# Dummy products on a constant tile, a clamp on ScalarE, and the sample rows' copies in a stream of their own: three small edits to a planned hybrid decoder layer

## The chip, the core and the metric

The kernel runs on one core of a Trainium2 chip. A core has five engines that run side by side: TensorE (PE: matrix products; its weight loads are shown apart as PEld), VectorE (DVE), ScalarE (ACT), GpSimd (POOL) and SyncE (SP), which here issues the transfers. The metric is the time of one execution on the device in microseconds (us); lower is better. Of several runs the median counts.

## The reference: one layer of a hybrid decoder

One layer is computed for a prompt of 1024 new tokens and, with the same weights, for 8 sample sequences of one new token each that bring their states along. The model width is 1024. The layer projects the input by a wide matrix `w_in`, feeds two branches, and merges them:

```python
p = x @ w_in
q, k, v, g_a, a_lr = gla part of p         # gated linear attention, 4 heads of 128 x 256
pr = p_rwkv + (prev - p_rwkv) * mu          # token shift, then RWKV-7, 16 heads of 64
r, kb, vb, g_b, w_lr, aa_lr = parts of pr
w = exp(-0.606531 * sigmoid(w0 + tanh(w_lr) @ w2));  a = sigmoid(a0 + aa_lr @ a2)
kk = kb * k_k
kk = kk / max(sqrt(sum(kk * kk per head)), 1e-12)
S_t = S_{t-1} (diag(w_t) - kk_t^T (kk_t * a_t)) + v_t^T k_t;   y_t = S_t r_t
m = sigmoid(gate_a) * (o_gla @ w_up_gla) + sigmoid(gate_b) * (o_rwkv @ w_up_rwkv)
y_out = layernorm(2**0.25 * x + m @ w_out)
```

All outputs are float32: the tokens' results, both branches' final states and the last projected row, for the prompt and for the samples. For this change three lines matter: the normalisation of `kk` with its lower bound, the product with `w_out` for the sample rows, and the fact that everything begins with the product by `w_in`.

## The kernel before

**Two passes.** The tokens are treated in two passes of 512 (line 29): pass 0 holds the first 512 prompt tokens and, behind them, the 8 sample tokens (columns 512 to 519, `HT:`); pass 1 the other 512. Data lie with channels on the 128 partitions and tokens along the row. A product in float32 is done as three products of shortened operands: each matrix is split into a high part (a cast on ScalarE) and a low part (the rest, a subtraction on VectorE), and high by high, high by low and low by high are summed. So the tiles `xh`, `xl` are the input's parts, 8 slices of each (`k`), and `wb` holds both parts of half a block of weights (from `wraw`).

**Blocks of products.** `blocks` (line 678) walks a list that `make_plan` wrote: for each block of 128 output columns and each slice `k` three products per column tile, then an evacuation out of PSUM by ScalarE and VectorE. After the projections of both passes come the up-projections, and at the end `out` (line 1554), the product by `w_out`, row block by row block, each followed by `out_part`: residual sum, layer norm and a transfer.

**Who sets the order.** The order on every engine is written out at build time. Each piece of work is a Python generator, a stream, that yields one step at a time. `Order.run` (line 368) keeps a model of when each engine and tile is free; in every round it looks at the next step of all streams and emits the one with the earliest start, less a bonus for the stream's kind (`PRIO`, line 77), plus a charge if the step needs another of ScalarE's function tables (`SETS`, line 84: Sigmoid and Tanh in one, Exp and Ln in another; functions outside that list are taken to need none). A table is loaded at line 392. Steps of `E` may go to VectorE or GpSimd and steps of `C` to ScalarE or VectorE, whichever the model has free first. The engines then run their own queues in that fixed order. A stream's next step is only considered once its last is emitted. Since almost all steps are emitted through one helper, the profile shows them under line 219 and they are told apart by their tiles.

**The start.** `setup` (line 485) makes the constant tiles and sets five bias columns (line 520) and the tile `reset` on VectorE, before the planner begins. The stream `warm` (line 1730) then takes a work tile `z` of 128 x 256, sets it to zero on VectorE and does three float32 products of it on TensorE, whose result nobody reads. In the trace each of them is two instructions, `big<-row`. Meanwhile the first slices of the input and of the weights land (`row<-xT`, `wraw<-w_in`), are split, and the first projections and the low-rank products (`big<-xh,war`, `low_rank`, line 731) begin. The tile `smp` (line 538) is allocated in `setup` and holds the sample rows of the token shift later on.

**A pair's front.** The RWKV heads are treated as 8 pairs per pass, so 16 times in all. `front` (line 1094) prepares a pair. It squares the keys (ScalarE), sums them per head by a product with a block matrix (`head_sums`, line 472, which yields a PSUM bank), clamps the sums from below to 1e-24 on VectorE into the tile `te` (line 1134), and takes the power of -1/2 by Ln and Exp on ScalarE (lines 1138 and 1139). In the trace the clamp is `TENSOR_SCALAR row<-big`, and the Exp is `row<-row,b_kkl`. Between the clamp and the Ln the stream yields a prefix scan on VectorE and a memset. The result is used by a product on VectorE with the tile `nkk`. After the front come a triangular inverse on VectorE and a chain of small products through the tokens.

**The sample rows of the output.** In pass 0, `out` sets in the row block of the 8 sample tokens as the second of five. It collects their columns of the high parts in columns 0 to 7 of a tile `both`, those of the low parts in columns 32 to 39, for each of the 8 slices, so that one pair of products serves both. In the first half of the output columns, each slice's two copies are yielded just before that slice's two products (lines 1583 and 1584), in the stream of the blocks itself; the second half finds them made.

Of the kernel before, what the change touches and what calls it, by code (L numbers as in the profile page):

```python
# [10 lines left out]
F32 = mybir.dt.float32  # L11
# [3 lines left out]
AF = mybir.ActivationFunctionType  # L15
ALU = mybir.AluOpType
# [4 lines left out]
P = 128  # L21
D = 1024
NK = D // P
TP = 1024
NS = 8
T = TP + NS
HT = TP // 2
# [4 lines left out]
NPAIR = RH // 2  # L32
# [61 lines left out]
KK_SCALE = 65536.0  # L94
# [318 lines left out]
class Kern(Order):  # L413
# [71 lines left out]
    def setup(self):  # L485
        nc, a = self.nc, self.a
        E = mybir.EngineType
        self.es.enter_context(self.tc.manual_schedule(engines={E.PE, E.Activation, E.DVE, E.Pool, E.SP}))
        cp = self.pool("const")
        wp = self.pool("w", side="left")  # L490
        self.dr = self.pool("dr", space=DRAM)
        pp = self.pool("psum", space=PSUM)
        xp = self.pool("x", side="right")
        self.r1 = r1 = self.pool("work", side="left")
        for tag, bufs in BANKS.items():
            self.buffers(tag, bufs, lambda tag=tag, bufs=bufs: pp.tile([P, 512], F32, name=tag, bufs=bufs))
        for tag, (shape, bufs) in SBUF.items():
            dt = F32R if tag in PARTS else F32
            self.buffers(tag, bufs, lambda tag=tag, shape=shape, bufs=bufs, dt=dt:
                         r1.tile(shape, dt, name=tag, bufs=bufs))  # L500
        for tag, (shape, bufs) in WBUF.items():
            dt = F32 if tag == "wraw" else F32R
            self.buffers(tag, bufs, lambda tag=tag, shape=shape, bufs=bufs, dt=dt:
                         wp.tile(shape, dt, name=tag, bufs=bufs))
        for k in range(NK):
            for v in "hl":
                tag = f"x{v}{k}"
                self.buffers(tag, 1, lambda tag=tag: xp.tile([P, HALF], F32R, name=tag, bufs=1))
        nc.scalar.preload_act_table_set(EXP)
        self.cons = cp.tile([P, CST_W], F32, name="cons")  # L510
        self.pv = cp.tile([P, PV_W], F32, name="pv")
        self.ident = self.cst("ident")
        self.omu = cp.tile([P, NRC], F32, name="omu")
        self.oka = cp.tile([P, 8], F32, name="oka")
        self.nkk = cp.tile([P, 8], F32, name="nkk")
        self.bias = {}
        for n, v in [("glaeps", GLA_EPS), ("gneps", GN_EPS), ("lneps", LN_EPS), ("one", 1.0),
                     ("kkl", 0.5 * math.log(KK_SCALE))]:
            t = cp.tile([P, 1], F32, name="b_" + n)
            nc.vector.memset(t, v)  # L520
            self.bias[n] = t
        dbg = getattr(self, "dbg", {})
        self.o_gla = dbg.get("o_gla", None) or self.dr.tile([D, T], F32, name="o_gla")
        self.o_rwkv = dbg.get("o_rwkv", None) or self.dr.tile([D, T], F32, name="o_rwkv")
        self.sg = [[[self.dr.tile([P, PASS[i][1]], F32, name=f"sg{i}{n}{k}") for k in range(NK)] for n in range(2)]
                   for i in range(2)]
        self.mg = [[self.dr.tile([P, PASS[i][1]], F32, name=f"mg{i}{k}") for k in range(NK)] for i in range(2)]

        self.lev = cp.tile([P, MASKED * 64 * NGC + P], U8, name="lev")

        self.onesr = cp.tile([P, P], F32R, name="onesr")
        self.headsr = cp.tile([P, P], F32R, name="headsr")
        self.war = cp.tile([P, NK * 32], F32R, name="war")
        self.alr = cp.tile([96, HALF], F32R, name="alr")
        self.gw2 = cp.tile([96, GH * GDK], F32R, name="gw2")
        self.GS = [self.dr.tile([P, GDV], F32, name=f"GS{h}") for h in range(GH)]

        self.smp = cp.tile([P, 4, NPAIR, NS], F32, name="smp")
        self.RS = self.dr.tile([4, NS, D], F32, name="RS")
        self.WA = self.dr.tile([2, NS, D], F32, name="WA")  # L540
        self.tail = cp.tile([P, NS + 1, NRC], F32, name="tail")
        self.carry = cp.tile([P, NRC], F32, name="carry")
        self.shT = cp.tile([P, NRC, NS], F32, name="shT")
        self.reset = cp.tile([P, HT], U8, name="reset")
        nc.vector.memset(self.reset, 1)
        nc.vector.memset(self.reset[:, ::C], 0)

        self.Sd = [self.dr.tile([P, C], F32, name=f"Sd{n}") for n in range(NPAIR)]

        for tag, n, bufs in (("az", 4 * HT, 2), ("XT", 2 * HT, 2), ("Lp", HT, 1), ("As", HT, 1)):  # L550
            ts = [cp.tile([P, n], F32, name=f"{tag}{i}") for i in range(bufs)]
            for t in ts if tag != "az" else []:
                nc.gpsimd.memset(t, 0.0)
            self.fixed(tag, ts)
# [539 lines left out]
    def front(self, c, p, st, d):  # L1094
        a, A, V, E = self.a, self.A, self.V, self.E
# [24 lines left out]
        ta, tb, td, te, Pc_ = yield from self.rows(5)  # L1120
        ta, tb, td, te = (x[:, :HT] for x in (ta, tb, td, te))
# [9 lines left out]
        yield A.activation(td, pa, AF.Sigmoid, bias=self.pvec("a0", p))  # L1131
        self.free(pa, l2)
        ps = yield from self.head_sums(te)
        yield V.tensor_scalar(te, ps, 1e-24, None, ALU.max)
        self.free(ps)
        yield V.tensor_tensor_scan(tb, self.reset, ta, 0.0, ALU.mult, ALU.add)
        yield E.memset(Pc[:, :, 0:1], 1.0)
        yield A.activation(te, te, AF.Ln, scale=KK_SCALE)
        yield A.activation(te, te, AF.Exp, scale=-0.5, bias=self.bias["kkl"])
        yield A.activation(Pc[:, :, 1:], bc(tb), AF.Exp, scale=-LAM)  # L1140
        yield A.activation(tb, tb, AF.Exp, scale=LAM)
# [13 lines left out]
        ps = yield from self.head_sums(te)  # L1155
# [398 lines left out]
    def out(self, c, xs):  # L1554


        rows = [(n * P, P, slice(0, P), c.i * HT + n * P) for n in range(HT // P)]
        if c.ns:
            rows.insert(1, (HT, C, slice(0, NS), TP))
            both_ = yield from self.row(NK * C)  # L1560
            both = both_.rearrange("p (k t) -> p k t", k=NK).bitcast(F32R)
            yield self.E.memset(both_, 0.0)
        for t0, m, ro, x0 in rows:
            fin = x0 == rows[-1][3]
            w = ro.stop - ro.start
            z_ = yield from self.get("XT")
            z = [z_[ro, :512], z_[ro, 512:]]
            for j in range(2):
                yield self.S.dma_start(z[j], self.a["x"][x0:x0 + w, 512 * j:512 * j + 512])
            st = yield from self.get("st")  # L1570
            end = fin and c.i
            parts = [(0, 512), (512, 256), (768, 256)] if end else [(0, 512), (512, 512)]
            for n, (c0, cn) in enumerate(parts):
                ps = yield from self.get_of("proj", "pY", "big")
                q = ps[:m, :cn]
                j, cs = c0 // 512, slice(c0 % 512, c0 % 512 + cn)
                for k in range(NK):
                    yield lambda: len(xs) > k and len(self.wo) > k
                    hi, lo = (x[j][:, cs] for x in self.wo[k])
                    xh, xl = xs[k]  # L1580
                    if x0 == TP:
                        if not n:
                            yield self.C.copy(both[:, k, 0:NS], xh[:, HT:])
                            yield self.C.copy(both[:, k, 32:32 + NS], xl[:, HT:])
                        yield self.P.matmul(q, both[:, k], hi, start=(k == 0), stop=False)
                        yield self.P.matmul(q, both[:, k], lo, start=False, stop=(k == NK - 1))
                        continue
                    yield self.P.matmul(q, xh[:, t0:t0 + m], hi, start=(k == 0), stop=False)
                    yield self.P.matmul(q, xh[:, t0:t0 + m], lo, start=False, stop=False)
                    yield self.P.matmul(q, xl[:, t0:t0 + m], hi, start=False, stop=(k == NK - 1))  # L1590
                    if fin and n == len(parts) - 1:
                        self.free(xh, xl)

                if x0 == TP and n == len(parts) - 1:
                    self.free(both_)
                self.spawn(self.out_part(n, len(parts), z, j, cs, ps, q[ro], st[ro], ro, x0, [z_, st]), "evacuate")
# [120 lines left out]
    def run_all(self):  # L1717
# [10 lines left out]
        self.make_plan()  # L1728

        def warm():  # L1730
            z = yield from self.row(2 * P)
            yield self.V.memset(z, 0.0)
            ps = yield from self.bank("big", [P, 2 * P])
            for n in range(3):
                yield self.P.matmul(ps, z[:, :P], z, start=True, stop=True)
            self.free(z, ps)
        self.spawn(warm(), "x")

        def samples():
# [59 lines left out]
```

## Time and profile before

| what | value |
|---|---|
| median of 3 runs | 1514.6 us (1512.83 to 1515.94) |
| the profiled execution | 1520.49 us |
| its span, first to last instruction | 1518.7 us |
| instructions | 31506 |
| TensorE products, weight loads | 1481.2 us, 1303.4 us busy |
| VectorE, ScalarE | 1125.9 us, 877.4 us busy |
| mean granted TensorE clock | 0.997 |

The profile shows, for one execution, when each instruction of each engine ran. A stretch row gives the busy time of the engines within a window; a wait row gives how long an engine stood idle and which engine's write of which tile ended that; a row of a group gives the count, total and mean duration of instructions of one shape, and the idle time before them; a timeline row gives the start, the duration and, in brackets, the idle time before it. In names like `row<-big` the written tile stands first; `row` is a general work tile, and `proj`, `big`, `pch` and `pY` are PSUM banks.

### The profile page before, as it was taken

The page shows a single profiled execution, that of the slowest core. Times are in us where ns is not written, and L with a number is a line of the kernel's source. Part 1 is how long each engine was busy: PE and PEld are TensorE (multiplying, and loading weights), DVE is VectorE, ACT ScalarE, POOL GpSimd, SP SyncE. Part 2 cuts the span into 40 slices and gives each one's busy share as a digit, 9 for nine tenths or more (in the row PEclk, how much of TensorE's full clock was granted, in tenths as well). Part 3 has the DMA queues.
Part 4 walks back from the last instruction along what each step waited for, and adds up shares of the span by engine and source line. Part 5 has one row for each costly group of instructions (what it writes and reads, how often), then busy time and mean ns, then how long its engine had stood idle before and what let it go on. Part 6 is the DMA issues. An engine that isn't in the chain of part 4 may idle for free.

```text
span 1518.7 us, 31506 instructions
## 1 busy us (share of the span) xinstructions
PE 1481.2 (98%) x11352; PEld 1303.4 (86%) x11352; DVE 1125.9 (74%) x2570; ACT 877.4 (58%) x2209; POOL 94.5 (6%) x273
## 2 busy tenths in 40 slices
PE   8999999999999999999999999899999999999997
PEld 7999999999999998877878777778788899988786
DVE  5687789786986698669778888776765775665665
ACT  5666677675677577566664555456546645554310
POOL 1010000000110000001001010200000000000000
PEclk9999999999999999999999999999999999999999
DMA  8768977789768976586576557555764778697622
GB/s 305 259 226 263 308 259 220 221 245 308 238 210 251 309 249 218 175 245 178 162 199 209 148 164 234 170 142 176 200 194 127 217 241 260 238 312 252 208 84 83
DMA packets 252823, 330.58 MB, mean 218 GB/s; under 512 B 125011, under 2 KB 148700, under 8 KB 252668
## 3 DMA queue, kind: packets, MB, share of 16 engines
q1 hardware_dynamic: 252668, 328.58, 69.7%
q8 instruction: 90, 1.47, 0.4%
q14 instruction: 65, 0.53, 0.1%
HBM read 198.35 MB, written 118.61 MB: 209 GB/s over the span
## 4 chain that ended last, share of the span: by engine, by line
PE 74%; DVE 13%; DMA 6%; ACT 3%; issue 2%; SPq 1%; POOL 0%; POOLq 0%; DVEq 0%; ACTq 0%
PE proj L219 45%; PE big L219 16%; PE pY L219 8%; DVE row L219 6%; PE pch L219 5%; DVE X L219 3%; ACT row L219 2%; SPq L219 1%; DVE wide L219 1%; DMA row<-sg 1%; DMA wide<-LD 1%; DVE part L219 1%; DMA w<-wb 1%; DVE pair L219 1%; DMA row<-state_rwkv 0%
## 5 line engine op out<-in xcount | busy, mean ns | idle before, releaser
L219 PE MATMUL proj<-xh,wb 128*128 128x256 f32 (+3 forms) x3744 | 912.7, 328 | 1.1 <-DVE row L219 0.8
L219 PEld LDWEIGHTS proj<-xh,wb 128*128 128x128 f32 x3744 | 624.4, 189 | 46.5 <-issue 2.6
L219 PE MATMUL proj<-xl,wb 128*128 128x256 f32 (+3 forms) x1872 | 612.1, 327 | 0.0
L219 PEld LDWEIGHTS proj<-xl,wb 128*128 128x128 f32 x1872 | 353.8, 189 | 23.2 <-issue 1.9
L219 DVE TENSOR_TENSOR wb<-wraw,wb 128x512 fp32r<-128x512 f32 x208 | 141.9, 689 | 78.1 <-ACT wb L219 74.3
L219 ACT CAST wb<-wraw 128x512 fp32r<-128x512 f32 x210 | 129.9, 622 | 90.3 <-PE proj L219 41.1
L219 DVE TENSOR_TENSOR row<-row 128x512 f32<-128x512 f32 (+8 forms) x338 | 166.1, 501 | 15.3 <-DMA row<-state_rwkv 6.4
L219 ACT ACTIVATE row<-row 128x512 f32<-128x512 f32 (+3 forms) x229 | 138.6, 611 | 36.2 <-DVE row L219 17.7
L219 DVE SCALAR_TENSOR_TENSOR wide<-pch,pc,s0p 64x64 f32<-64x64 f32 x224 | 63.1, 281 | 51.9 <-PE pch L219 46.9
L219 PE MATMUL big<-row 128*128 128x128 f32 (+4 forms) x466 | 87.1, 322 | 9.0 <-DVE row L219 4.1
L219 ACT ACTIVATE row<-proj,omu 128x256 f32<-128x256 f32 (+1 forms) x99 | 54.2, 548 | 68.6 <-PE proj L219 67.6
L219 ACT COPY rh<-pch 128x128 f32<-128x128 f32 x118 | 31.4, 266 | 105.6 <-PE pch L219 104.3
L219 DVE TENSOR_REDUCE X<-X 128x54 f32<-128x162 f32 (+14 forms) x256 | 85.4, 334 | 6.4
L219 ACT ACTIVATE s0p<-wide,pc 64x64 f32<-64x64 f32 x256 | 88.9, 347 | 1.8
L219 POOL TENSOR_TENSOR row<-row 128x256 f32<-128x256 f32 (+6 forms) x47 | 42.5, 909 | 688.0 <-DVE row L219 435.6
L219 DVE SCALAR_TENSOR_TENSOR row<-proj,pv,row 128x255 f32<-128x255 f32 (+1 forms) x99 | 56.4, 570 | 35.3 <-ACT tail L219 25.4
L219 PEld LDWEIGHTS big<-row 128*128 128x128 f32 (+3 forms) x466 | 59.5, 178 | 21.1 <-ACT row L219 7.0
L219 DVE TENSOR_TENSOR X<-X,wide 128x108 f32<-128x108 f32 (+14 forms) x256 | 71.2, 278 | 6.6
L392 ACT ACT_TABLE_LOAD x58 | 74.4, 1283 | 1.0
L219 PE MATMUL big<-xh,wb 128*128 128x512 f32 (+2 forms) x272 | 69.2, 332 | 2.9 <-ACT wb L219 2.6
L219 ACT COPY row<-big 128x128 f32<-128x128 f32 (+5 forms) x145 | 43.3, 317 | 38.4 <-PE big L219 35.5
L219 PE MATMUL pY<-xh,wb 128*128 128x256 f32 (+2 forms) x256 | 63.2, 326 | 0.0
(269 smaller groups left out, 2324.8 us busy)
## 6 DMA issues: line engine op xcount, KB each, us to landing
w<-wb SPq DMA_DIRECT2D x146, 512.0 KB
wb<-w SPq DMA_DIRECT2D x146, 512.0 KB
wraw<-w_in SPq DMA_DIRECT2D x146, 256.0 KB
wide<-LD SPq DMA_DIRECT2D x64, 128.0 KB
wraw<-w_up_gla SPq DMA_DIRECT2D x32, 256.0 KB
wraw<-w_up_rwkv SPq DMA_DIRECT2D x32, 256.0 KB
sg<-row SPq DMA_DIRECT2D x16, 260.0 KB
row<-sg SPq DMA_DIRECT2D x16, 260.0 KB
```

The source lines that it names most:

```text
L219: ways.append((eng, lambda call=call: call(out, *args, **kw), price(eng, name, out, args, ins)))
L392: self.nc.scalar.preload_act_table_set(self.table)
```

## The change

Three edits. The tile `smp` is allocated and set to zero at the beginning of `setup`, and `warm` uses it in place of a work tile of its own, for five products and not three. The clamp of the squared keys' sums becomes a Relu on ScalarE with a bias of -1e-24, and the Ln behind it gets that amount back as a bias, multiplied by its scale, so that the value is the same; two bias columns are added for that. In `out`, the copies of the sample rows move into a stream of their own of kind "x", which yields them as soon as each input slice is there; the products wait until the planner has emitted their slice's copies.

```diff
@@ setup
+        self.smp = cp.tile([P, 4, NPAIR, NS], F32, name="smp")
+        nc.vector.memset(self.smp.rearrange("p n c b -> p (n c b)"), 0.0)
         self.bias = {}
         for n, v in [("glaeps", GLA_EPS), ("gneps", GN_EPS), ("lneps", LN_EPS), ("one", 1.0),
-                     ("kkl", 0.5 * math.log(KK_SCALE))]:
+                     ("kkl", 0.5 * math.log(KK_SCALE)), ("kkn", -1e-24), ("kke", 1e-24 * KK_SCALE)]:
...
-        self.smp = cp.tile([P, 4, NPAIR, NS], F32, name="smp")
@@ front
         ps = yield from self.head_sums(te)
-        yield V.tensor_scalar(te, ps, 1e-24, None, ALU.max)
+        yield A.activation(te, ps, AF.Relu, bias=self.bias["kkn"])
         self.free(ps)
         yield V.tensor_tensor_scan(tb, self.reset, ta, 0.0, ALU.mult, ALU.add)
         yield E.memset(Pc[:, :, 0:1], 1.0)
-        yield A.activation(te, te, AF.Ln, scale=KK_SCALE)
+        yield A.activation(te, te, AF.Ln, scale=KK_SCALE, bias=self.bias["kke"])
@@ out
             yield self.E.memset(both_, 0.0)
+            there = []
+
+            def gather():
+                for k in range(NK):
+                    yield lambda: len(xs) > k
+                    for n, x in enumerate(xs[k]):
+                        yield self.C.copy(both[:, k, 32 * n:32 * n + NS], x[:, HT:])
+                    there.append(k)
+            self.spawn(gather(), "x")
...
                     if x0 == TP:
-                        if not n:
-                            yield self.C.copy(both[:, k, 0:NS], xh[:, HT:])
-                            yield self.C.copy(both[:, k, 32:32 + NS], xl[:, HT:])
+                        yield lambda: len(there) > k
                         yield self.P.matmul(q, both[:, k], hi, start=(k == 0), stop=False)
@@ warm
-            z = yield from self.row(2 * P)
-            yield self.V.memset(z, 0.0)
+            z = self.smp.rearrange("p n c b -> p (n c b)")
             ps = yield from self.bank("big", [P, 2 * P])
-            for n in range(3):
+            for n in range(5):
                 yield self.P.matmul(ps, z[:, :P], z, start=True, stop=True)
-            self.free(z, ps)
+            self.free(ps)
```

## The prediction

> **What bounds the kernel now.** I read the page first (engines' busy time), then busy time by stretches, the list of TensorE's waits, the groups by shape and last the timeline around the three edited places. The page's first row and the stretches:
>
> ```profile
> PE 1481.2 (98%) x11352; PEld 1303.4 (86%) x11352; DVE 1125.9 (74%) x2570; ACT 877.4 (58%) x2209; POOL 94.5 (6%) x273
> ```
> ```profile
> 6.47:10.37 3.90, 3.90 (x18) 3.37 (x19) 3.39 (x7) 3.07 (x6) 0.61 (x5) 1.00 0.97 316
> 10.37:18.00 7.63, 7.51 (x62) 6.90 (x60) 4.82 (x11) 3.56 (x7) 0.00 (x0) 1.00 0.89 330
> 100.00:400.00 300.00, 298.21 (x2864) 286.85 (x2863) 240.10 (x576) 203.44 (x543) 16.88 (x64) 1.00 0.80 254
> 400.00:600.00 200.00, 194.97 (x1852) 185.37 (x1851) 165.91 (x393) 143.92 (x369) 15.98 (x49) 1.00 0.76 247
> 600.00:800.00 200.00, 197.09 (x1343) 159.66 (x1343) 147.26 (x364) 125.65 (x317) 10.75 (x35) 1.00 0.69 195
> 800.00:1000.00 200.00, 188.93 (x1289) 151.72 (x1288) 167.61 (x383) 100.99 (x266) 23.81 (x49) 0.99 0.63 181
> 1000.00:1240.00 240.00, 235.36 (x1646) 196.54 (x1645) 164.54 (x400) 138.38 (x354) 13.71 (x45) 0.99 0.64 187
> 1240.00:1424.90 184.90, 184.62 (x1194) 164.18 (x1194) 111.11 (x198) 98.36 (x202) 2.10 (x2) 1.00 0.77 251
> 1424.90:1429.02 4.12, 4.07 (x18) 2.00 (x17) 3.13 (x7) 1.67 (x9) 0.00 (x0) 1.00 0.66 224
> 1507.00:1518.70 11.70, 3.92 (x34) 3.71 (x32) 5.86 (x12) 0.50 (x2) 2.77 (x3) 0.87 0.18 67
> ```
>
> The columns are the stretch, its length, then busy time of PE, PEld, DVE, ACT and POOL, granted clock, DMA share and GB/s. TensorE is busy for 1481.2 of 1518.7 us, so only 37.5 us can be won without taking products away. Of those, 7.8 us (11.70 less 3.92) lie behind the last products and are untouched. From 100 to 1240 us the five rows leave 1.8 + 5.0 + 2.9 + 11.1 + 4.6 = 25.4 us idle. The rest is at the start. In the idle middle the waits are many and short (total, times, longest):
>
> ```profile
> PE pch L219 <- DVE wide L219: 4.6, 5, 2.0
> PE big L219 <- DVE part L219: 3.5, 5, 1.4
> PE big L219 <- ACT wb L219: 2.6, 1, 2.6
> PE big L219 <- ACT row L219: 2.4, 3, 1.3
> PE pch L219 <- ACT wide L219: 2.3, 2, 1.5
> PE big L219 <- DVE row L219: 2.1, 5, 0.8
> ```
>
> No wait is longer than 2.6 us. These rows give 10.2 us behind VectorE and 7.3 us behind ScalarE: neither engine owns the loss.
>
> **The change, part by part. First the dummy products.** The timeline of the start:
>
> ```profile
> 0.79 0.06 DVE L520 MEMSET b_glaeps<- 128x1 f32 x1 [0.79 <-PEq L1791]
> 1.67 0.27 DVE L219 MEMSET row<- 128x256 f32 x1
> 1.99 2.93 PE L219 MATMUL big<-row 128*128 128x256 f32 x6 [1.99 <-DVE row L219]
> 4.11 0.70 DVE L219 TENSOR_TENSOR xl<-row,xh 128x520 fp32r<-128x520 f32 x1 [2.17 <-ACT xh L219]
> 4.76 0.58 PE L219 MATMUL proj<-xh,wb 128*128 128x256 f32 x1
> 5.38 0.34 DVE L219 CAST war<-row 128x128 fp32r<-128x128 f32 x1 [0.57 <-DMA row<-wa]
> 6.47 0.42 PE L219 MATMUL big<-xh,war 128*32 128x256 f32 x1 [1.13 <-DVE war L219]
> 7.26 2.00 DVE L219 TENSOR_TENSOR xl<-row,xh 128x520 fp32r<-128x520 f32 x3
> ```
>
> Removed: one DVE memset of 0.27 us inside the planned order. Added: the same memset ahead of everything on VectorE, two bias memsets of 0.06 us, and two more products, so ten instead of six PE instructions. Behind the earlier memset on its engine stand the bias and reset memsets; VectorE then idles 2.17 us before 4.11, which covers all of it. The first dummy started 0.32 us after its memset (1.67 to 1.99), so it can now start at 0.79 + 0.32, near 1.1 us. Ten instructions at 2.93/6 = 0.49 us end by 6.0 us at the latest. That pushes the first real product back from 4.76 by up to 1.2 us, but TensorE stood idle for 1.13 us before 6.47, waiting for a VectorE cast that a DMA released at 5.38 and the step after it, and that wait stays. Cover gone would cost about 0.1 us, the difference.
>
> What can be won is speed. From 6.47 to 10.37 us 18 products took 3.90 us, 0.217 each; from there to 18.00, 62 took 7.51, 0.121 each. (The granted clock reads 1.00 in both rows: that column doesn't show this half speed.) If the longer dummy run brings the fast rate to 6.47, 18 x (0.217 - 0.121) = 1.7 us go. Not all: the second slice of the input has its low part at 7.26 + 2.00/3 = 7.93, and the first slice's nine products would end at 6.47 + 9 x 0.121 = 7.56; about 0.4 us of waiting comes back, leaving 1.3. The bounds are 1.3 won and 0.1 lost; I take 0.8 won, nearer to the gain, because the idle 1.13 us between the early work and 6.47 shrinks to some 0.4, while the fast rate came 3.9 us after the last such gap. TensorE is then bound by its own work, so the gain lasts.
>
> [...]
>
> **Second, the clamp.** Groups by shape (count, busy us, mean ns, idle before), and one of the sixteen places in the timeline:
>
> ```profile
> L219 DVE TENSOR_SCALAR row<-big 128x512 f32<-128x512 f32 x16 | 11.0, 689 | 7.5 <-PE big L219 7.4
> L219 ACT ACTIVATE row<-big,b_gneps 128x512 f32<-128x512 f32 x16 | 11.0, 689 | 4.0 <-PE big L219 3.8
> L219 ACT ACTIVATE row<-row 128x512 f32<-128x512 f32 x136 | 85.2, 631 | 26.2 <-DVE row L219 14.9 <-DMA row<-sg 10.2
> L219 ACT ACTIVATE row<-row,b_kkl 128x512 f32<-128x512 f32 x16 | 11.6, 722 | 0.3
> L392 ACT ACT_TABLE_LOAD x58 | 74.4, 1283 | 1.0
> ```
> ```profile
> 1091.38 0.69 DVE L219 TENSOR_SCALAR row<-big 128x512 f32<-128x512 f32 x1
> ...
> 1092.20 1.28 ACT L392 ACT_TABLE_LOAD   x1
> 1093.49 0.63 ACT L219 ACTIVATE row<-row 128x512 f32<-128x512 f32 x1
> ```
>
> VectorE loses 16 x 0.689 = 11.0 us. The trace has no Relu; its nearest row is the other activation of that shape that reads PSUM with a bias column, also 0.689. The logarithm behind it gains a bias column: 0.722 - 0.631 = 0.091. ScalarE thus gains 16 x 0.78 = 12.5 us. On the path the step is neutral: in this place the logarithm comes 1.4 us after the clamp's end (1091.38 + 0.69 to 1093.49), because a table load stands between, and a Relu ahead of that load takes the same 0.69 us. Behind it on ScalarE are queued evacuations of projections and halves of weights, on which TensorE's next blocks wait; on VectorE the scan and the rows behind the clamp come 0.69 us earlier.
>
> What of 11.0 less and 12.5 more reaches TensorE the trace can't show. The best case is that the waits on VectorE's parts and rows go, 3.5 + 2.1 = 5.6 us; the worst, that all 12.5 stand in front of a product. The planner also shares out the copies that either engine can do by their loads, so part of the added work returns. ScalarE has more room (143.92 against 165.91 busy in 400 to 600, 100.99 against 167.61 in 800 to 1000), and I take 0.5 us won.
>
> Every step after the first clamp is placed anew, since the planner picks the earliest step each time. That order has no price. Stretches of similar work lose between 2.9 (600 to 800) and 5.0 (400 to 600) per 200 us, so a new draw may well shift the 25.4 us by three to five either way; I take zero.
>
> **Third, the sample rows.**
>
> ```profile
> 1424.90 1.07 PE L219 MATMUL proj<-gg,row 128*64 128x512 f32 x4
> 1429.02 1.09 PE L219 MATMUL big<-gg,row 128*64 128x512 f32 x4
> 1432.71 0.62 PE L219 MATMUL pY<-gg,xh 128*128 128x512 f32 x2
> ```
> ```profile
> 1426.92 0.19 PEld L219 LDWEIGHTS proj<-row 128*64 128x64 f32 x2 [0.52 <-DVE row L219]
> 1427.56 0.19 PEld L219 LDWEIGHTS proj<-row 128*64 128x64 f32 x2 [0.45 <-ACT row L219]
> L219 ACT CAST row<-xl 128x8 fp32r<-128x8 f32 x7 | 1.3, 193 | 0.0
> ```
>
> The 16 products of the first half take 1429.02 - 1424.90 = 4.12 us, those of the second, which need no copies, 3.69. So the copies' late issue costs 0.43 us, and their own stream gives that back. The products still wait for their copies; behind a waiting one on TensorE stand the other row blocks of the output, but by then the copies are done. The 16 copies, up to 0.193 us each, 3.1 in all, move ahead to where the input slices are made, before 1424.90. There TensorE is busy 184.62 of 184.90 us, with whole blocks of products queued; that is the cover, and without it up to 3.1 us would be late.
>
> Sum: 0.8 + 0.5 + 0.4 = 1.7 us. The profiled execution took 1520.5 us, 1.8 more than its span of 1518.7, so it would become 1518.8. The median of the runs is 1514.6, 5.9 lower; microseconds carry over one to one, giving 1512.9.
>
> **The rivals.** *VectorE's relief reaches TensorE.* For it: VectorE is the fuller engine from 200 us on, and the rows name it for 10.2 us. Against: the clamps themselves were not late. With half to all of the 5.6 us, and 1.2 from the other two parts, it gives 1514.6 - 4.0 = 1510.6 down to 1507.8.
>
> *ScalarE becomes late, the time is slower.* Place: the Relu and the longer logarithm in the pairs' fronts, ahead of evacuations. Price: 12.5 us, of which half in front of products costs 6.2, less 1.2 won elsewhere: 1519.6. It decides against me from a share of 4.2/12.5, a third, for then the loss passes 3.0 us net. For it: the three rows with ScalarE already hold 7.3 us. Against: ScalarE's shares above. [...]
>
> *The dummies don't bring the fast rate forward.* Then 1514.6 - 0.9 = 1513.7; for it speaks that the start has 0.4 us of idle left.
>
> *The Relu isn't among the loaded functions.* Each would then bring a table load: 16 x 1.283 = 20.5 us on ScalarE, with half on the path 1524. The plan treats it like Copy and Square, which share every table here, so I hold it unlikely.
>
> **How the numbers follow.** A measurement of this kernel can tell about 0.2%, 3.0 us, from no change. Forecast, 1512.9: 0.37. Dummies without effect, 1513.7: 0.04. VectorE's relief: 0.36. ScalarE late: 0.20. Table loads: 0.03. So faster 0.36, same 0.41, slower 0.23. The range runs from the relief's far end, 1507.0 with a good draw of the order, to ScalarE's 1519.6, leaving out under 2 in 10. The forecast's own range is 1511.6 to 1517.
>
> **What would show it.** Right: ten dummy instructions from about 1.1 us, products 0.12 us apart soon after 6.47; sixteen Relus of 0.69 us on ScalarE and still about 58 table loads; the sample block's halves both near 3.7 us; some 25 us idle between 100 and 1240 us. Wrong: fewer than 22 or more than 29 us idle there, the fast rate again after 10 us, or gaps from 1409 to 1425 where ScalarE copies.

## The result: slower by 0.68%, and the profile after

The changed kernel takes 1526.9 us (median of 4 runs, 1524.7 to 1528.7) against 1514.0 us for the one before (4 runs, 1512.8 to 1515.9). The ratio is 1.0068, with a 95% interval of 1.0052 to 1.0084: 12.9 us by the two medians, or 10.3 us by the ratio. The second figure is the better one: in the later jobs the median of before was 1516.4 to 1517.0 us. The forecast was 1512.9 with a range up to 1519.6. Two profiled executions show less of it: 1520.49 us before, 6.5 above its median, and 1524.67 after, 2.3 below its own. So the two profiles can account for 4.2 us only, and what follows from them is tested with timed runs.

The page's first row and the stretches of after (columns as in the prediction):

```profile
PE 1484.6 (97%) x11356; PEld 1306.4 (86%) x11356; DVE 1106.9 (73%) x2538; ACT 884.0 (58%) x2228; POOL 107.5 (7%) x284
```
```profile
6.47:10.37 3.90, 3.90 (x32) 3.55 (x31) 3.56 (x7) 3.04 (x6) 0.57 (x5) 1.00 0.95 308
...
100.00:400.00 300.00, 297.99 (x2846) 285.27 (x2846) 228.67 (x548) 207.08 (x554) 15.57 (x63) 1.00 0.79 253
400.00:600.00 200.00, 194.28 (x1839) 185.56 (x1838) 162.73 (x396) 144.96 (x379) 18.35 (x55) 0.99 0.71 232
600.00:800.00 200.00, 196.97 (x1315) 158.12 (x1314) 135.49 (x329) 119.41 (x292) 12.43 (x35) 1.00 0.68 196
800.00:1000.00 200.00, 192.48 (x1272) 154.63 (x1271) 164.62 (x388) 102.89 (x277) 31.27 (x55) 1.00 0.66 193
1000.00:1240.00 240.00, 230.06 (x1660) 192.19 (x1659) 170.41 (x405) 139.63 (x350) 18.07 (x47) 0.99 0.63 183
```

The start did what was forecast: 32 products from 6.47 to 10.37 us where 18 ran before. It is no accident of one execution: over all profiles of this document that window holds 27 to 33 products in the ten kernels with five dummies, and 18 to 23 in the eight with three, except for one with 31 (`v_plus20`). VectorE has 19.0 us less work, ScalarE 6.6 more, so the planner has also shared out the copies anew. In the middle, from 100 to 1240 us, TensorE is idle for 2.0 + 5.7 + 3.0 + 7.5 + 9.9 = 28.2 us, against 25.4 before.

The three edits, each in its place (timeline of the start; groups by shape; timeline of the sample block):

```profile
0.85 0.27 DVE L517 MEMSET smp<- 128x256 f32 x1 [0.85 <-PEq L1798]
1.18 4.63 PE L219 MATMUL big<-smp 128*128 128x256 f32 x10 [1.18 <-DVE smp L517]
6.28 0.42 PE L219 MATMUL big<-xh,war 128*32 128x256 f32 x1 [0.26 <-DVE war L219]
```
```profile
L392 ACT ACT_TABLE_LOAD x54 | 69.3, 1283 | 0.9
L219 ACT ACTIVATE row<-row,b_kke 128x512 f32<-128x512 f32 x16 | 11.6, 727 | 0.1
L219 ACT ACTIVATE row<-big,b_kkn 128x512 f32<-128x512 f32 x16 | 11.0, 688 | 4.1 <-PE big L219 3.9
```
```profile
1429.50 1.09 PE L219 MATMUL big<-gg,row 128*64 128x512 f32 x4
...
1433.20 1.09 PE L219 MATMUL big<-gg,row 128*64 128x512 f32 x4
```

Ten dummy instructions start at 1.18 and close the idle time ahead of 6.28 to 0.26 us. Sixteen Relus cost 688 ns each and the logarithm 727, as estimated, and no table loads were added (54 beside 58). The sample block's first half now takes 1433.20 - 1429.50 = 3.70 us, not 4.12. These terms came out as priced; the loss is elsewhere.

### The profile page after: what moved, and what is told of

It reads as the page before. It is cut to its first block, busy times and chain, and to the rows that moved or that the text cites. A ratio compares the mean times of both kernels' runs of the same rounds, so it can differ in the third digit from the quotient of the medians.

```text
span 1522.9 us, 31527 instructions
## 1 busy us (share of the span) xinstructions
PE 1484.6 (97%) x11356; PEld 1306.4 (86%) x11356; DVE 1106.9 (73%) x2538; ACT 884.0 (58%) x2228; POOL 107.5 (7%) x284
## 4 chain that ended last, share of the span: by engine, by line
PE 50%; DVE 14%; ACT 3%; DMA 3%; issue 2%; SPq 1%; POOL 0%; POOLq 0%; DVEq 0%; ACTq 0%
PE proj L219 26%; PE big L219 14%; PE pY L219 8%; DVE row L219 5%; DVE X L219 4%; PE pch L219 2%; DVE wide L219 2%; ACT row L219 2%; DMA wide<-LD 1%; SPq L219 1%; DVE pair L219 1%; DVE wb L219 0%; DVE part L219 0%; DVE az L219 0%; DMA rwkv_p<-sto 0%
## 5 line engine op out<-in xcount | busy, mean ns | idle before, releaser
L219 DVE TENSOR_TENSOR row<-row 128x256 f32<-128x256 f32 (+9 forms) x334 | 163.7, 499 | 16.9 <-ACT row L219 5.5
L219 ACT ACTIVATE row<-row 128x512 f32<-128x512 f32 (+4 forms) x213 | 128.4, 610 | 15.9 <-DVE row L219 9.2
L219 POOL TENSOR_TENSOR row<-row 128x256 f32<-128x256 f32 (+6 forms) x51 | 50.2, 987 | 568.2 <-DVE row L219 356.6
L219 ACT COPY row<-big 128x128 f32<-128x128 f32 (+6 forms) x145 | 43.1, 317 | 41.1 <-PE big L219 40.1
L219 PE MATMUL pY<-xh,wb 128*128 128x264 f32 (+2 forms) x256 | 63.6, 321 | 0.0
```

Source lines behind the costliest of these rows:

```text
L219: ways.append((eng, lambda call=call: call(out, *args, **kw), price(eng, name, out, args, ins)))
```

## The experiments

The planner prices each step and then emits it, so the price and the instruction can be separated. A kernel can be told the old clamp's price and engine and yet emit the Relu (the order stays that of before), or the reverse. Another can run unchanged instructions under a slightly wrong price (the order is drawn anew). All ratios are to the kernel before, run on the same chip in the same job, with 95% intervals.

**Order or engine?** The edit that pins the order:

```diff
-        yield V.tensor_scalar(te, ps, 1e-24, None, ALU.max)
+        op = V.tensor_scalar(te, ps, 1e-24, None, ALU.max)
+        relu = lambda: self.nc.scalar.activation(te, ps, AF.Relu, bias=self.bias["kkn"])
+        op.ways = [(e, relu, c) for e, _, c in op.ways]
+        yield op
```

and likewise for the Ln. First the second edit of the change alone (`e2_clamp`):

> The clamp and its logarithm alone are changed, as in the kernel after; dummies and sample rows stay as before. The planner then writes another order: 3007 of the lines of TensorE's 8216-line order differ from before. Theory O (the loss comes from the newly drawn order) and theory A (the loss comes from ScalarE's 12.5 us of added work) both expect nearly all of the 12.9 us: 1524 to 1529. Theory X (the loss comes from the other two edits) expects 1511 to 1517.

Measured: 1526.8 us, ratio 1.0067 (1.0054 to 1.0080). The clamp's edit alone brings the whole loss; the other two edits are cleared.

The same instructions with the order pinned (`e4_pinned`; in its trace all 11352 products stand in the order of before):

> The clamp runs on ScalarE and the logarithm has its bias, but the planner is told the price and engine of the old clamp, so that the order of TensorE, GpSimd and the transfers is that of before to the line; on ScalarE the Relu stands where the planner emitted the clamp. Theory O expects the time of before within 3 us, 1511 to 1517. Theory A expects the loss to stay, 1523 to 1529.

Measured: 1520.6 us, ratio 1.0023 (1.0013 to 1.0034), 3.5 us. Two thirds of the loss go with the order.

The reverse, after's order with the clamp back on VectorE (`e5_back`, the diff above with the roles exchanged):

> The reverse: all three edits are in and the planner is told of the Relu, so the order of TensorE and the transfers is that of the kernel after to the line, but the clamp runs on VectorE and the logarithm has no bias. Theory O expects the time of after, 1523 to 1529. Theory A expects the loss to go, 1511 to 1516.

Measured: 1525.4 us, ratio 1.0053 (1.0040 to 1.0066). Without a Relu on ScalarE the order alone keeps 0.53 of the 0.68%. Theory A falls as the main cause, theory O stands.

**What is wrong with that order?** Over 80 us the largest difference of the two profiles lies around 580 us; from 1000 to 1080 us it is nearly as large. Stretches of before:

```profile
540.00:560.00 20.00, 20.00 (x161) 19.65 (x160) 18.38 (x45) 17.38 (x38) 1.87 (x3) 1.00 0.93 301
560.00:580.00 20.00, 19.09 (x174) 18.30 (x174) 19.84 (x45) 15.38 (x39) 1.31 (x1) 1.00 0.88 286
580.00:600.00 20.00, 19.20 (x192) 16.80 (x191) 17.62 (x43) 13.49 (x34) 2.69 (x11) 1.00 0.58 195
600.00:620.00 20.00, 20.00 (x116) 16.87 (x116) 12.83 (x35) 12.14 (x38) 0.65 (x4) 1.00 0.54 159
```

and of after:

```profile
540.00:560.00 20.00, 18.34 (x208) 17.24 (x202) 18.08 (x42) 15.51 (x35) 3.81 (x6) 1.00 0.75 229
560.00:580.00 20.00, 19.16 (x145) 18.61 (x143) 18.03 (x45) 14.83 (x37) 3.39 (x12) 0.91 0.65 213
580.00:600.00 20.00, 17.54 (x181) 15.95 (x180) 14.39 (x36) 13.86 (x39) 0.32 (x1) 1.00 0.19 73
600.00:620.00 20.00, 19.56 (x175) 16.55 (x175) 12.35 (x27) 12.16 (x31) 1.50 (x4) 1.00 0.87 265
```

TensorE is busy for 74.6 of 80 us and not 78.3, and in the second row its clock falls to 0.91. (The rows compare the same microseconds, not the same work: the products in them differ.) The timeline of after on VectorE and on TensorE there:

```profile
557.96 1.20 DVE L219 TENSOR_TENSOR_SCAN row<-reset,row 128x512 f32<-128x512 uint8 x1
559.07 0.34 DVE L219 COPY row<-row 128x128 f32<-128x128 f32 x2
```
```profile
557.61 0.28 PE L219 MATMUL proj<-xl,wb 128*128 128x264 f32 x1
559.55 0.77 PE L219 MATMUL big<-row 128*128 128x128 f32 x4 [1.66 <-DVE row L219]
```

and the clock in the three stretches around it:

```profile
556.00:559.55 3.55, 1.89 (x26) 1.52 (x25) 3.52 (x9) 3.38 (x8) 0.27 (x3) 1.00 1.02 338
560.00:563.40 3.40, 3.40 (x19) 3.40 (x18) 3.04 (x9) 1.89 (x4) 0.00 (x0) 0.50 0.73 228
563.40:566.80 3.40, 3.40 (x31) 3.40 (x31) 2.17 (x6) 2.09 (x6) 0.67 (x1) 0.99 0.02 8
```

The front's prefix scan, which follows the clamp in its stream, stands on VectorE just ahead of two small copies for a GLA head, and TensorE's next product waits for those: 1.66 us. Then the clock is 0.50 for 3.4 us: 19 products where the next 3.4 us have 31, by estimate some 1.3 us more (12 of 31 of 3.4). That second part doesn't appear as idle time at all: the row from 560.00 has TensorE busy for 3.40 of 3.40 us. With the clamp back on VectorE in the same order (`e5_back`), the clamp stands there too, and the wait is longer (in a profiled execution that was the slowest of its six, 1532.7 us):

```profile
561.93 0.72 DVE L1136 TENSOR_SCALAR row<-big 128x512 f32<-128x512 f32 x1
562.57 1.21 DVE L219 TENSOR_TENSOR_SCAN row<-reset,row 128x512 f32<-128x512 uint8 x1
563.69 0.34 DVE L219 COPY row<-row 128x128 f32<-128x128 f32 x2
```
```profile
564.17 0.69 PE L219 MATMUL big<-row 128*128 128x128 f32 x4 [2.31 <-DVE row L219]
```

This is one place. The longest single wait of after lies at another, 1225 us:

```profile
1228.71 0.27 ACT L219 COPY sto<-big 99x128 f32<-99x128 f32 x1 [4.57 <-DMA rwkv_p<-sto]
1229.03 0.79 PE L219 MATMUL big<-part,headsr 128*128 128x512 f32 x1 [3.55 <-ACT sto L219]
```

TensorE waits 3.55 us for a copy on ScalarE, but ScalarE had itself stood idle for 4.57 us, until a transfer out of the tile `sto`, of which there is one, was done. So this isn't ScalarE's load either, and `e5_back` has the same wait without a Relu (3.9 us). The rest of the profile's loss is spread over many shorter places; which choices of the planner led to each wasn't traced.

**Are orders with a Relu bad, or is this one draw?** Eight kernels draw a new order by a wrong price of the clamp, four with the instructions of before and four with all three edits:

```diff
-        yield V.tensor_scalar(te, ps, 1e-24, None, ALU.max)
+        op = V.tensor_scalar(te, ps, 1e-24, None, ALU.max)
+        op.ways = [(e, f, c + 0.02) for e, f, c in op.ways]
+        yield op
```

(0.02, -0.02, 0.05 and -0.05; the same with the Relu's line.) What was expected of them:

> The instructions of before, the clamp on VectorE, but the planner is told that the clamp costs 0.02 us more than it did. Nothing that runs has changed except the order (2199 differing lines of TensorE's 8216). Theory L (before's order is one good draw among many, so any new draw costs some us) expects slower than before by 2 to 12 us. Theory S (the loss belongs to the Relu's place on ScalarE in the plan) expects before within 3 us.

> The instructions of before with the clamp's price in the plan 0.02 us lower: a third new draw of the order with the clamp on VectorE (2658 differing lines on TensorE). Theory L expects slower than before by 2 to 12 us, theory S before within 3 us.

> As the last, with the clamp's price in the plan 0.05 us lower (2997 differing lines on TensorE). Theory L expects slower than before by 2 to 12 us, theory S before within 3 us.

> The instructions of before, the clamp's price in the plan 0.05 us higher: a draw near before's (965 differing lines on TensorE). By the scatter of the other draws, between 0.4% faster and 0.4% slower than before.

> All three edits with the Relu's price in the plan 0.02 us higher: a further draw with the clamp on ScalarE (2441 lines on TensorE differ from after, 3118 from before). Theory L expects a time within the spread of the other draws, theory S after's loss, 8 to 13 us.

> All three edits with the Relu's price in the plan 0.02 us lower (2546 lines on TensorE differ from after). Theory L expects a time within the spread of the other draws, theory S after's loss, 8 to 13 us.

> All three edits, the clamp on ScalarE, with the Relu's price in the plan 0.05 us lower (3088 lines on TensorE differ from after, 2961 from before). Theory L expects another draw: anywhere from 2 us faster to 15 us slower than before, not bound to after's time. Theory S expects after's loss again, 8 to 13 us.

> All three edits, the Relu's price in the plan 0.05 us higher (1858 lines on TensorE differ from after, the nearest draw to it). If draws with a Relu in the plan are bad on average, 0.5% slower than before or more; if draws only scatter, anything from 0.6% faster to 0.7% slower, and after's own trouble spots would be back only where the order is the same.

Measured:

| price in the plan | before's instructions | all three edits |
|---|---|---|
| right | 1 (before) | 1.0068 (after) |
| +0.02 us | 0.9971 (0.9960 to 0.9983) | 0.9936 (0.9922 to 0.9949) |
| -0.02 us | 0.9972 (0.9960 to 0.9984) | 1.0011 (1.0001 to 1.0022) |
| +0.05 us | 1.0038 (1.0025 to 1.0052) | 0.9991 (0.9979 to 1.0003) |
| -0.05 us | 1.0018 (1.0008 to 1.0027) | 0.9979 (0.9970 to 0.9989) |

Both theories fall. Theory S: of four new draws with the Relu, two are clearly faster than before, one is level and one slower by 0.11%. Theory L: before isn't a good draw either, two of four new draws of its own instructions beat it by 0.3%. The two columns have means of 1.0000 and 0.9997. Over all ten the standard deviation is 0.38%, or 5.7 us, and the span 1.32%. After is the slowest of the ten and its neighbour in price the fastest: 1507.5 us against 1517.0 for before in that job. That version, all three edits with the Relu's price 0.02 us higher in the plan, beats both kernels. Its page and middle:

```profile
PE 1476.1 (98%) x11356; PEld 1300.9 (87%) x11356; DVE 1102.1 (73%) x2535; ACT 891.7 (59%) x2237; POOL 101.1 (7%) x282
```
```profile
100.00:400.00 300.00, 298.76 (x2863) 286.78 (x2862) 231.89 (x560) 207.07 (x558) 19.00 (x66) 1.00 0.80 253
400.00:600.00 200.00, 195.50 (x1839) 185.26 (x1839) 153.88 (x364) 144.29 (x369) 14.89 (x47) 1.00 0.76 246
600.00:800.00 200.00, 196.28 (x1343) 158.74 (x1342) 150.69 (x380) 125.22 (x315) 16.75 (x43) 1.00 0.69 193
800.00:1000.00 200.00, 196.53 (x1360) 160.71 (x1358) 171.02 (x406) 113.34 (x296) 27.37 (x66) 1.00 0.65 191
1000.00:1240.00 240.00, 236.78 (x1718) 198.77 (x1715) 161.52 (x377) 143.88 (x348) 11.30 (x30) 1.00 0.65 192
```

ScalarE is fuller here than in after (891.7 against 884.0 us), yet TensorE is idle for 16.2 us in the middle and not 28.2, and the clock reads 1.00 in every row.

**What the clamp's engine costs by itself.** Two more kernels exchange the engine within a drawn order:

> The order of a_plus20 to the line on TensorE, all three edits in the plan, but the clamp runs on VectorE and the logarithm without a bias. If the place on ScalarE costs 2 to 3 us by itself, as the two pairs so far say, 0.8% faster than before, 2 us better than a_plus20's 0.64%. If it costs nothing, the same 0.64% within the interval.

Measured: ratio 0.9950 (0.9934 to 0.9966). a_plus20, the same order with the Relu, had 0.9936 in another job: here ScalarE comes out better, if anything.

> The order of v_plus20 to the line on TensorE, with the clamp as a Relu on ScalarE and the logarithm's bias, and the dummies and copies of before. If the place on ScalarE costs 2 to 3 us, 0.1 to 0.15% faster than before and not 0.29%. If it costs nothing, 0.29% again.

Measured: ratio 0.9980 (0.9967 to 0.9993) beside 0.9971 for v_plus20. And all three edits in before's order, beside the same without the clamp:

> All three edits, but the planner is told the old clamp's price and engine, so that the order of before stays but for 70 lines of TensorE near the output. If the terms add up: the pinned clamp alone was 0.23% slower than before, the dummies 0.08% faster, the copies at most 0.03% faster, so 0.1% slower, 1 to 3 us. If the new order were not the main loss, it would be near after, 0.5% slower or more.

> The dummies and the sample rows' own stream, without the clamp. The order differs from before only near the output (70 lines on TensorE). Expected from the prediction's terms: 0.8 and 0.4 us won, 0.1% faster than before; if the copies bring nothing, the same as the dummies alone, 0.08% faster.

Measured: 1.0014 (1.0003 to 1.0025) and 1.0002 (0.9993 to 1.0010). With the first pairs, the five differences in one order are +0.23, +0.15, +0.09, -0.14 and +0.12%, on average 0.09% or 1.4 us for the place on ScalarE. In before's order it costs some 2 to 3.5 us (the interval of the second pair just reaches zero); in the others the intervals overlap and even the sign isn't settled.

**The dummies alone:**

> The dummies alone: five on the constant tile; every engine's order is that of before apart from the dummies and the memset. The prediction's term expects 0.8 us won, with bounds of 1.3 won and 0.1 lost: 1512.7 to 1514.1. The rival that the dummies don't bring the fast rate forward expects 1514.0.

Measured: ratio 0.9992 (0.9981 to 1.0003). That is 1.2 us won, close to the term, with an interval that touches zero; with the copies added (`e6_warm_copies`) nothing can be seen.

## Why the prediction was wrong

**The step that failed** is the last one of the clamp's part: "Every step after the first clamp is placed anew [...] That order has no price [...] a new draw may well shift the 25.4 us by three to five either way; I take zero." Zero was right as a mean: the ten draws average within 0.03% of before, with a standard error of 1.8 us. The size was wrong. The bound came from two neighbouring stretches' idle time; measured, a draw has a standard deviation of 5.7 us (4.6 without after itself) and went from 9.7 us faster to 10.3 slower. Besides, the range gave the term room on one side only: a good draw lengthens the faster end, and no bad draw the slower one, which is ScalarE's price alone. With the measured size a range of eight in ten, 1.28 standard deviations, reaches 7.3 us to either side, 1505.6 to 1520.2. The outcome lies beyond even that, as the worst of ten draws may.

**Idle time was a narrow measure, though not an empty one.** My sign of a failure was more than 29 us idle from 100 to 1240 us. After has 28.2. The same five rows in the profiles of the ten draws leave from 16.2 us (`a_plus20`, the fastest) to 29.3 (`v_plus50`, the slowest with the old instructions), against 25.4 in before: 9.3 less to 3.9 more, where the prediction allowed three to five. Beside these 13.1 us stand 20.8 us between the two profiled times (1504.98 and 1525.83), so a draw works in good part through such waits. The wait of 1.66 us in after cost more than its length, since the 3.4 us at a clock of 0.50 behind it, with 19 products and not 31, are counted as busy. But before's profile has two such stretches, 3.4 us at 0.50 from 952.44 and from 1232.34, as after's has, from 560.03 and from 1229.04; and the mean clock of `v_plus50`'s profiled execution is 0.999, where two such stretches alone would take off 0.2% (3.4 of 1524 us). So they don't explain the loss. What made up the rest stays open.

**The rival on the slower side** had the direction and a near time, 1519.6, but the wrong mechanism. It put the loss in ScalarE's 12.5 us. After's order keeps 0.53 of the 0.68% with the clamp on VectorE, and the fastest draw has ScalarE fuller than after (891.7 against 884.0 us). Of the four longest rows of TensorE's waits in after (total, times, longest), ScalarE has one, 3.6 us at the single place shown above:

```profile
PE big L219 <- DVE row L219: 9.9, 14, 1.9
PE big L219 <- ACT sto L219: 3.6, 1, 3.6
PE pch L219 <- DVE wide L219: 3.5, 6, 1.0
PE big L219 <- DVE S L219: 2.4, 5, 0.8
```

VectorE has 19 us less to do, and the row behind its general tiles still went from 4.1 us (2.0 of it at the start, for the dummies' memset) to 9.9. Here a fuller or emptier engine said little; at the places that were traced, a copy's position behind a scan or a transfer did.

**Right were these terms**: ten dummies from 1.1 us (measured 1.18) and the fast rate by 7 us (measured: 0.21 us from product to product until 7.12, then 0.12; 1.2 us won, not clear of zero, against 0.8); the Relu at 0.69 us and the logarithm's 0.09; no added table loads; the copies' 0.4 us in the trace, too small for the timed runs. The half microsecond credited to VectorE's relief wasn't found; the five pairs give 1.4 us of cost instead.

## What to carry to other kernels

Where a greedy planner writes the order, any edit that changes a price or an engine early on is first of all a new draw. Measure the draw's scatter by wrong prices under unchanged instructions before judging the edit, and judge the edit inside a pinned order. A change worth 1 us can't be accepted or refused from one build whose order scatters by 5.7 us; but a handful of draws is itself a cheap search, here worth 0.64%, or 0.50% in the second kernel with that order.

## What was unexpected of the hardware

Behind some short stalls of these runs the granted clock was 0.50 for 3.4 us, so that the stall in after cost more than its 1.66 us: 19 products and not 31 in the 3.4 us from 560.00. In before:

```profile
949.00:952.40 3.40, 1.23 (x6) 0.88 (x6) 3.32 (x7) 2.65 (x8) 0.00 (x0) 1.00 0.40 150
952.40:955.80 3.40, 3.40 (x54) 2.89 (x57) 3.37 (x6) 0.00 (x0) 0.34 (x1) 0.51 0.35 71
...
1228.90:1232.30 3.40, 1.72 (x12) 1.51 (x13) 3.29 (x9) 2.46 (x5) 0.00 (x0) 1.00 0.68 182
1232.30:1235.70 3.40, 3.40 (x18) 3.40 (x17) 3.23 (x11) 0.00 (x0) 0.00 (x0) 0.50 0.66 219
```

Behind each of these two stretches of 3.4 us, in which TensorE was busy for 36 and 51% of the time, the granted clock is 0.50 to 0.51 for the next 3.4 us and 1.00 again behind that. It didn't always happen. In the same execution the clock stays at 1.00 behind a stretch with 49%, in which one wait took 2.03 us (before 978.13):

```profile
976.40:979.80 3.40, 1.67 (x10) 1.48 (x10) 3.10 (x10) 1.43 (x5) 0.00 (x0) 1.00 0.38 141
979.80:983.20 3.40, 3.40 (x18) 2.65 (x17) 3.24 (x11) 1.97 (x5) 0.00 (x0) 1.00 0.44 129
```

It happened at a start too: with three dummies, `e2_clamp`'s execution idled for 1.65 us before its first low-rank product, and behind that the clock was 0.50 from 8.50 to 11.90 us, with 16 products in 3.40 us:

```profile
5.00:8.40 3.40, 1.66 (x11) 1.17 (x11) 2.34 (x7) 1.33 (x3) 1.80 (x11) 1.00 0.97 306
8.50:11.90 3.40, 3.40 (x16) 2.78 (x17) 2.81 (x5) 2.63 (x5) 0.00 (x0) 0.50 1.02 350
```

So the five dummies' use may lie as much in the closed gap as in the longer run; this wasn't tried apart. (In before the column reads 1.00 from 6.47 to 10.37 us, where the products came 0.217 us apart, as the prediction notes; these later stretches it shows.) Gaps of 1.65 and 1.66 us, in stretches with TensorE busy for 49% (1.66 of 3.40 us) and 53% (1.89 of 3.55), stood ahead of a clock of 0.50; the 2.03 us in a stretch with 49% did not. What decides between them isn't shown.
